# Matrix product with batch normalisation on one core: a fifth chunk copied apart, the last half chunk whole, and other durations in the planner

## The chip, the core and the metric

The kernel runs on one core of a Trainium2 chip. Five engines of that core take part, each with its own queue of instructions that it works off in order: TensorE (PE, with PEld for its weight loads), VectorE (DVE), ScalarE (ACT), GpSimd (POOL) and SyncE (SP, which only issues transfers). The metric is the device time in microseconds; 7 runs of the kernel before have the median 210.38 us.

## The reference

```python
y = np.matmul(x, weight)                       # x (16, 512, 1024) float32, weight (1024, 768)
mean = np.mean(y, axis=(0, 1), keepdims=True)
var = np.var(y, axis=(0, 1), keepdims=True)
y_norm = (y - mean) / np.sqrt(var + eps)
return (gamma * y_norm + beta).astype(np.float32)
```

So 8192 rows of 1024 are multiplied into 768 columns, and each column is normalised by its mean and variance over all 8192 rows. No column can be stored before its last row is computed.

## The kernel before

**Tiles.** The 8192 rows are 16 chunks of 512 (`CH`), called c0 to c15 here. The 768 columns are six blocks of 128, called b0 to b5 (`nt` in the code). K is cut into 8 slices of 128: 4 values of `jw` times 2 of `e`, so one chunk of one block takes 8 matrix instructions.

**Load phase.** GpSimd issues the loads of x (`load_x`, L386), four transfers for a chunk, which turn float32 into bf16 on the way into a buffer called `ring` that holds three chunks. VectorE transposes them into `xT` tiles: L414 moves pairs of bf16 as one float32, so that the two `e` planes stay interleaved; L407, for the chunks in `SINGLE` (c2, c3, c6), moves single bf16 and leaves the planes apart. TensorE computes b0 and b1 with x as the stationary operand (`rows_unit`, L480; two units of 16 instructions for a chunk, each into one PSUM bank) for c0 to c13. For c14 and c15 it does them the other way round (`ga_unit`, L782). Each unit of `rows_unit` is worked off by three engines: ACT squares it (L626), VectorE adds it to `sum1` (L629), ACT keeps it in bf16 (L639), and the square is added either by GpSimd to `sum2` or by VectorE to `sum3` (`add_squares`, L633, both). After the last unit the sums are folded (`tot`, L763 and L768) and a few small matmuls (L840) bring them across the partitions.

**Column blocks.** b2 to b5 have w as the stationary and x as the moving operand (`col_unit`, L545, 8 instructions of 512 columns). c0 to c3 do them in the load phase; c4 to c15 do them after it, block by block, b2 first. The result in PSUM is read by VectorE for its statistics (`bn_stats`, L678) and by ACT, which keeps it in bf16 (L682). When a block has all its chunks, its scale and shift are computed (`finish_tasks`), and eight pieces of 1024 rows are normalised (L1005), turned back (by a transposing transfer, L1107, or on TensorE, L1023) and stored by SP (L1089). The 8 units of PSUM are handed out in turn, so the ninth unit waits until the first one has been kept.

**Copies apart.** `part_chunk` (L517) copies an interleaved `xT` chunk into two planes `x_pl`, four instructions of 128x1024 for a chunk. ACT does that for the chunks in `PARTED` during the load. For the chunks in `LATE` (c12 to c15) it is done by GpSimd or VectorE, whichever the planner picks, once b3 of the last late chunk has been kept; the planes then serve b4 and b5. The twelve `xT` slots are all taken at that time, so a copy goes into the slot of a chunk that has been copied already; the first late chunk (`i == 0`) goes into small free tiles instead. In b3 the late chunks come first, in b4 they come last (`CHUNKS`); a late chunk draws its neighbour of the pair with it.

**The end.** The last block of the last chunk (`last_unit`, L720) is computed in the three pieces of `PIECES` (256, 128 and 128 columns), each with its own statistics (L727) in `fin`. Then come the last scale and shift (L1166 to L1178), the normalisation of b5 (L1201), the turning (L1023), the copy out of PSUM (L1214) and eleven stores (L1217).

**What sets the order.** Nothing runs in the order in which the program names it. Every piece of work is a `task` with a due time, the engines that may do it and for each engine a duration; `arrange` then plays the whole kernel through once while it is built, always gives the engine that is free first the ready task that is due first, and writes the instructions down in that order. Each engine's queue is thus fixed by the durations in the code, and on the chip it is worked off in that order, whatever the durations are there. A task with two engines goes to the one that the planner sees free first. A task with `lock` is kept apart from GpSimd's in the planner when VectorE does it.

Of the kernel before, what the change touches and what calls it, by code (L numbers as in the profile page):

```python
# [227 lines left out]
def kernel(  # L228
# [15 lines left out]
    B, M0, K = x.shape  # L244
# [3 lines left out]
    P = 128  # L248
    NT = N // P
    KQ = K // 4  # L250
    CH = 512
    RT = CH // P
    C = M // CH
    QR = 256
    QPC = CH // QR
    JW = KQ // 64
    PIECES = ((0,QR),(QR,P),(QR+P,P))
    WAKE = 8
    FILL = 2
    EARLY = 4  # L260
# [1 line left out]
    GA = 2  # L262
    NA = GA * P
    GY = 2
    PAD = 34
    HELD = 1
    ASTAT = {2:tuple(range(4,16))}
    RC = C - 2
    XT, YB, SQ = C - EARLY, 27, 3
    ADDED = (0,6,16,28,40)  # L270
    PARTED, LATE, SINGLE = (4,5,7,8,9,10), (12,13,14,15), (2,3,6)
    MODE = {2:'xact',3:('xact',)*7+('pe',),4:'pe'}
    MODE = {nt: m if isinstance(m, tuple) else (m,) * (C // GY) for nt, m in MODE.items()}
    RING = 3 * CH // 32 * KQ // 2
# [46 lines left out]
    tot = singles.tile([P, 2, NA], f32)  # L321
    stats = singles.tile([P, (NT - GA) * C + PAD, 6], f32)
    fin = singles.tile([P, 9 + 6 * len(PIECES)], f32)
    psums = {nt: singles.tile([P, 2, C], f32, name=f"psums{nt}") for nt in ASTAT}
# [20 lines left out]
    def task(prio, engines, emit, deps=(), lock=False, **kw):  # L345
        t = Task(prio, engines, emit, deps, **kw)
        t.lock = lock
        tasks.append(t)
        return t
# [13 lines left out]
    LINE, PER_KB = 0.00119, 1 / 385.0  # L363
# [16 lines left out]
    def load_x(m0, rows, slot):  # L380
        def emit(eng):
            x_bf = piece(slot).bitcast(bf16).rearrange("p (t k) -> p t k", k=KQ)
            slot.tile = x_bf
            src = x_flat[m0:m0 + rows].rearrange("(t r) k -> r t k", r=32)
            for i in range(4):
                seq(nc.gpsimd.dma_start(x_bf[32 * i:32 * i + 32], src[:, :, KQ * i:KQ * (i + 1)]))  # L386
        return emit
# [34 lines left out]
    t = 1.0  # L422
    affine = None
    for kind, n, *n1 in order:
        if kind == "w":
            took = 4 * 192 * 4 * (n1[0] - n) / 4 * PER_KB * 1.024
            w_ready[n] = task(t, {"POOL": (2.0, 2.0)}, load_w(n, *n1), dma=took)
            w_ready[n].count = 4
            t += 2.1 * (n1[0] - n)
            if n1[0] == JW:  # L430
                task(t, {"POOL": (0.6, 0.6)}, lambda eng: make_identity(nc, ident))
            continue
        rows = n1[0] if kind == "p" else QR if kind == "x" else CH
        m0 = n if kind == "p" else n * rows
        if m0 == M // 2:
            affine = task(t, {"SP": (5.0, 7.0)}, load_affine, [x_ready[m0 // CH - 3, 0, JW]])
        slot = Slot(rings, rows // 32 * KQ // 2)
        load = task(
            t, {"POOL": (2.55, 2.55)}, load_x(m0, rows, slot), dma=rows * K * 4 / 1024 * PER_KB * 1.024,
            takes=[slot])  # L440
        load.count = 4
        t += 2.7 * rows / QR
        for i in range(rows // QR):
            c, q = divmod(m0 // QR + i, QPC)
            for j0, j1 in ((0, JW // 2), (JW // 2, JW)) if m0 < CH else ((0, JW),):
                new = q == 0 and j0 == 0
                x_ready[c, q, j1] = task(
                    -1000 + t, dve((2.2 if c in SINGLE else 1.16) * (j1 - j0) / JW + 0.02),
                    turn_x(slot, x_slot[c], m0, i * QR // 32, j0, j1, new), [load],
                    uses=[slot] if new else [slot, x_slot[c]], takes=[x_slot[c]] if new else [])  # L450
                if not new:
                    x_ready[c, q, j1].deps.append(x_ready[c, 0, JW // 2 if m0 < CH else JW])
            x_ready.setdefault((c, q, JW // 2), x_ready[c, q, JW])
        if rows % QR:
            t0 = rows // QR * QR // 32
            m1 = m0 + 32 * t0
            c, q = divmod(m1 // QR, QPC)
            x_ready["tile", m1 // P] = task(
                -1000 + t, dve(0.63), turn_x(slot, x_slot[c], m0, t0, 0, JW, False, P),
                [load, x_ready[c, 0, JW]], uses=[slot, x_slot[c]])  # L460
            x_ready[c, q, JW] = x_ready[c, q, JW // 2] = x_ready["tile", m1 // P]
# [36 lines left out]
    def part_chunk(c, now, engines, small=False, step=0.0, after=()):  # L498

        src = x_slot[c]  # L500
        slots = [Slot(sqs if jw < SQ else ys) for jw in range(JW)] if small else [Slot(xts)] * JW
        ts = []

        def copy(jw):
            def emit(eng):
                if small:
                    if jw < SQ:
                        x_pl = sqpool.tile([P, 2, CH], bf16, tag="sq")
                    else:
                        x_pl = ypool.tile([P, 2, CH], bf16, tag="y")  # L510
                    slots[jw].tile = [x_pl]
                elif jw == 0:
                    x_pl = xtpool.tile([P, JW, 2, CH], bf16, tag="xT")
                    slots[0].tile = [x_pl[:, i] for i in range(JW)]
                dst = slots[jw].tile[0 if small else jw]
                pairs = src.tile[:, jw].rearrange("p m e -> p e m")
                seq(nc.scalar.copy(dst, pairs) if eng == "ACT" else ENG[eng].tensor_copy(dst, pairs))  # L517
            return emit

        for jw in range(JW):  # L520
            new = small or jw == 0
            ts.append(task(
                now + step * jw, engines, copy(jw), [x_ready[c, q, JW] for q in range(QPC)] + list(after) + ([] if new else ts[:1]),
                uses=[src] + ([] if new else [slots[jw]]), takes=[slots[jw]] if new else []))
        plain[c] = slots, ts, small

    def moving(c, jw, e, r0, r1, parted):
# [36 lines left out]
    clock = [12.0]  # L564
# [51 lines left out]
    def rows_stats(c, ts, slot, t):  # L616
        now = clock[0]
        h = ts[0] * P // QR
        sq_slot = Slot(sqs)
        state = {}  # L620
        n = len(ts) * NA

        def square(eng):
            sq_sb = sqpool.tile([P, 2 * NA], f32, tag="sq")
            state["sq"] = sq_sb
            seq(nc.scalar.activation(sq_sb[:, 0:n], slot.tile[:, 0:n], AF.Square))  # L626

        def add_rows(eng):
            seq(nc.vector.tensor_add(sum1, slot.tile[:, 0:n], sum1))  # L629

        def add_squares(eng):
            acc = sum2 if eng == "POOL" else sum3
            seq(ENG[eng].tensor_add(acc, acc, state["sq"][:, 0:n]))  # L633

        def keep(eng):
            if "y" not in y_row[c].__dict__:
                y_sb = ypool.tile([P, RT, NA], bf16, tag="y")
                y_row[c].y = y_sb
            seq(nc.scalar.copy(  # L639
                y_row[c].y[:, ts[0]:ts[0] + len(ts)].rearrange("p s n -> p (s n)"), slot.tile[:, 0:n]))  # L640

        new = ts[0] == 0
        kw = {"uses": [slot] + ([] if new else [y_row[c]]), "takes": [y_row[c]] if new else []}
        up = 0 if c < RC - 1 else now
        a = task(now + 3.0 - up, act(0.494), square, [t], uses=[slot], takes=[sq_slot])
        b = task(now + 3.2 - up, dve(0.608), add_rows, [a], uses=[slot])
        s = task((now + 4.2 if c < RC - 2 else 0), {"POOL": (1.23, 1.28), "DVE": (0.608, 0.7)}, add_squares, [a],
                 True, uses=[sq_slot])
        k = task(now + 3.4, act(0.48), keep, [b], **kw)
        row_end[c, ts[0]] = a, b, s, k  # L650
# [59 lines left out]
    def last_unit(q):  # L710
        nt, c = NT - 1, C - 1
        r0, rows = PIECES[q]
        slot = Slot(banks)
# [420 lines left out]
    for nt in range(GA, NT - 1):  # L1134
        if nt == NT - 2:
            for i, c in enumerate(LATE):
                part_chunk(c, clock[0] + 0.0 + 4.0 * i, {"POOL": (1.3, 1.35), "DVE": (1.1, 1.2)},
                           i == 0, 4.0 / 4, [col_end[NT - 3, late[-1]][1]])
        for c in CHUNKS[nt]:
            for jws in halves if nt > GA or c > EARLY + 2 else [[jw] for jw in range(JW)]:  # L1140
                col_unit(nt, c, jws)
        f = finish_tasks(nt)
        start = clock[0] + 3.0
        for i in range(C // GY):
            if nt == NT - 2 and C // GY - HELD <= i:
                held.append((nt, GY * i, f))
                continue
            col_block(nt, GY * i, start + STEP[nt] * i, f)
# [3 lines left out]
    for c in range(EARLY, C - 1):  # L1152
        for jws in halves:
            col_unit(nt, c, jws)
    for q in range(len(PIECES)):
        last_unit(q)
# [35 lines left out]
    for c, r0, rows in ends:  # L1192
# [5 lines left out]
        for i in range(n):  # L1198
            def norm_part(eng, c=c + i, r0=r0, rows=min(rows, CH)):
# [5 lines left out]
                              uses=[y_of(nt, c + i)]))  # L1205
        m0 = c * CH + r0
        count = rows // P
        b, bank = turn_block(due + 0.6 * (n - 1), nt, m0, count, norms, [y_of(nt, c + i) for i in range(n)])
        slot = Slot(xts)
# [6 lines left out]
        def store(eng, slot=slot, m0=m0, count=count):  # L1216
# [6 lines left out]
             uses=[slot])  # L1223
# [41 lines left out]
```

## Time and profile before

| what | value |
|---|---|
| median of 7 runs | 210.38 us (208.95 to 211.29) |
| the profiled execution | 209.6 us, span 207.8 us |
| busy: PE, DVE, ACT, POOL | 92%, 75%, 70%, 57% of the span |
| granted clock of TensorE | 0.974 of full speed, lower only after 190 us |
| 26 to 93 us (x still loading) | PE busy 66.20 of 67.00 us, DVE 61.53, POOL 54.43, 194 GB/s |
| 93 to 101 us (end of the load) | PE busy 7.65 of 8.00 us, POOL 7.55 |
| 112 to 165 us (b2, b3, b4) | PE busy 52.67 of 53.00 us, DVE 47.41, POOL 34.14, 302 GB/s |
| 165 to 190 us (b5) | PE busy 24.83 of 25.00 us, 305 GB/s |
| L633 on POOL, on DVE | 22 of 1301 ns, 6 of 836 ns |
| L517 on POOL, on DVE | 9 of 1201 ns, 7 of 899 ns |

A line of the timeline gives the start, the length, the engine, the line of the code, the operation and how many equal instructions it joins; in brackets stands how long the engine sat idle before it and for what. A line of the chain of work that ended last gives the start, the length, and what ran. The rates are those of what was moved, and a load is counted by its bf16 side.

### The profile page before, as it was taken

The page shows a single profiled execution, that of the slowest core. Times are in us where ns is not written, and L with a number is a line of the kernel's source. Part 1 is how long each engine was busy: PE and PEld are TensorE (multiplying, and loading weights), DVE is VectorE, ACT ScalarE, POOL GpSimd, SP SyncE. Part 2 cuts the span into 40 slices and gives each one's busy share as a digit, 9 for nine tenths or more (in the row PEclk, how much of TensorE's full clock was granted, in tenths as well). Part 3 has the DMA queues.
Part 4 walks back from the last instruction along what each step waited for, and adds up shares of the span by engine and source line. Part 5 has one row for each costly group of instructions (what it writes and reads, how often), then busy time and mean ns, then how long its engine had stood idle before and what let it go on. Part 6 is the DMA issues. An engine that isn't in the chain of part 4 may idle for free.

```text
span 207.8 us, 3502 instructions
## 1 busy us (share of the span) xinstructions
PE 192.2 (92%) x1217; PEld 117.2 (56%) x1232; DVE 156.1 (75%) x241; ACT 144.6 (70%) x252; POOL 118.4 (57%) x139
## 2 busy tenths in 40 slices
PE   7998989999999999999999999999999999997900
PEld 3465554656588888776865444444444455545900
DVE  4221889999999989878889999589999496248800
ACT  2001561368979999998888777989767969876940
POOL 7987954787499999999303999469830000000000
PEclk9999999999999999999999999999999999999675
DMA  5999999999999999999304898999999999999997
GB/s 64 161 198 189 195 196 196 196 197 196 190 193 197 197 196 195 192 172 188 45 0 156 313 342 306 155 356 341 327 269 280 274 317 325 320 281 347 330 347 238
DMA packets 94082, 47.69 MB, mean 229 GB/s; under 512 B 19824, under 2 KB 93552, under 8 KB 94064
## 3 DMA queue, kind: packets, MB, share of 16 engines
q0 software_dynamic: 34688, 18.36, 64.7%
q1 hardware_dynamic: 59376, 29.11, 51.5%
q8 instruction: 9, 0.15, 0.3%
q14 instruction: 9, 0.07, 0.1%
HBM read 36.71 MB, written 25.17 MB: 298 GB/s over the span
## 4 chain that ended last, share of the span: by engine, by line
PE 75%; DMA 10%; ACT 4%; issue 3%; POOL 2%; DVE 2%; ACTq 0%; DVEq 0%; POOLq 0%
PE y_ps L545 48%; PE y_ps L480 20%; DMA ring<-in_x_dram 8%; ACT o_sb L1214 3%; DMA w_sb<-in_weight_dram 3%; PE y_ps L782 2%; PE o_ps L1023 2%; DVE xT_sb L414 1%; POOL ring L386 1%; PE y_ps L720 1%; POOL tot L768 1%; PE a_ps L887 0%; ACTq L1260 0%; PE o_ps L1053 0%; POOL tot L763 0%
## 5 line engine op out<-in xcount | busy, mean ns | idle before, releaser
L545 PEld LDWEIGHTS <-w_sb 128*128 128x128 bf16 x512 | 49.6, 97 | 57.7
L545 PE MATMUL y_ps<-xT_sb,w_sb 128*128 128x512 bf16 (+1 forms) x255 | 59.3, 377 | 0.5
L545 PE MATMUL y_ps<-x_pl,w_sb 128*128 128x512 bf16 x242 | 57.6, 379 | 0.3
L386 POOL DMA_DIRECT2D ring<-in_x_dram x76 | 47.3, 628 | 12.3 <-DVE xT_sb L407 5.6
L480 PE MATMUL y_ps<-w_sb,xT_sb 128*128 128x256 bf16 x448 | 50.7, 273 | 1.4 <-DVE xT_sb L414 0.8
L480 PEld LDWEIGHTS <-xT_sb 128*128 128x128 bf16 x448 | 43.7, 98 | 9.6 <-issue 1.7
L414 DVE STREAM_TRANSPOSE xT_sb<-ring 128x1024 f32<-128x1024 f32 (+1 forms) x29 | 31.2, 1112 | 13.1 <-DMA ring<-in_x_dram 12.3
L678 DVE BATCH_NORM_STATS2 stats<-y_ps 128x6 f32<-128x512 f32 x46 | 30.8, 683 | 11.4 <-PE y_ps L545 9.7
L682 ACT CAST y_sb<-y_ps 128x512 bf16<-128x512 f32 x51 | 29.1, 589 | 14.2 <-DVE stats L678 8.1
L921 POOL TENSOR_TENSOR ring<-ring,sum 128x1024 f32<-128x1024 f32 (+1 forms) x11 | 23.7, 2177 | 17.1 <-DVE ring L916 16.4
L626 ACT ACTIVATE sq_sb<-y_ps 128x512 f32<-128x512 f32 x28 | 16.9, 608 | 23.5 <-PE y_ps L480 22.2
L633 POOL TENSOR_TENSOR sum<-sum,sq_sb 128x512 f32<-128x512 f32 x22 | 28.6, 1301 | 3.2 <-ACT sq_sb L626 2.4
L517 ACT COPY x_pl<-xT_sb 128x1024 bf16<-128x1024 bf16 x24 | 24.1, 1051 | 1.8 <-DVE xT_sb L414 1.8
L629 DVE TENSOR_TENSOR sum<-y_ps,sum 128x512 f32<-128x512 f32 x28 | 18.9, 675 | 7.9 <-ACT sq_sb L626 6.7
L1023 PE MATMUL o_ps<-ident,y_sb 128*128 128x128 bf16 x136 | 20.1, 241 | 1.7 <-DVE y_sb L1201 1.5
L916 DVE TENSOR_TENSOR ring<-y_sb,a_ps 128x1024 f32<-128x1024 bf16 (+1 forms) x16 | 16.8, 1079 | 2.8 <-DMA out_dram<-ring 2.8
L639 ACT CAST y_sb<-y_ps 128x512 bf16<-128x512 f32 x28 | 15.8, 593 | 3.0 <-DVE sum L629 2.9
L1119 ACT CAST ring<-ring 128x1024 f32<-128x1024 bf16 x15 | 15.7, 1052 | 1.4 <-DMA ring<-y_sb 1.4
L407 DVE STREAM_TRANSPOSE xT_sb<-ring 128x2048 bf16<-128x2048 bf16 x6 | 13.5, 2282 | 0.2 <-DMA ring<-in_x_dram 0.2
L1023 PEld LDWEIGHTS <-y_sb 128*128 128x128 bf16 x136 | 11.7, 109 | 3.3 <-DVE y_sb L1201 1.9
L517 POOL COPY x_pl<-xT_sb 128x1024 bf16<-128x1024 bf16 x9 | 10.5, 1201 | 3.9 <-DVE x_pl L517 3.1
L561 PE MATMUL idle_ps<-idle_sb 128*128 128x512 f32 x20 | 11.2, 717 | 1.5 <-DVE idle_sb L311 1.5
(92 smaller groups left out, 146.7 us busy)
## 6 DMA issues: line engine op xcount, KB each, us to landing
out_dram<-ring SPq DMA_DIRECT2D x38, 512.0 KB, 4.0
ring<-in_x_dram POOLq DMA_DIRECT2D x52, 256.0 KB, 8.5
out_dram<-o_sb SPq DMA_DIRECT2D x6, 512.0 KB, 5.2
ring<-in_x_dram POOLq DMA_DIRECT2D x16, 128.0 KB, 5.1
out_dram<-ring SPq DMA_DIRECT2D x4, 256.0 KB, 3.0
w_sb<-in_weight_dram POOLq DMA_DIRECT2D x8, 96.0 KB, 4.5
w_sb<-in_weight_dram POOLq DMA_DIRECT2D x4, 192.0 KB, 5.1
ring<-in_x_dram POOLq DMA_DIRECT2D x4, 192.0 KB, 8.2
```

Of the source, the lines that this page charges most:

```text
L386: seq(nc.gpsimd.dma_start(x_bf[32 * i:32 * i + 32], src[:, :, KQ * i:KQ * (i + 1)]))
L414: seq(nc.vector.transpose(dst, src[:, :, jw0:jw1]))
L480: seq(nc.tensor.matmul(y_ps[:, s], x_of(c, jw, e, t * P, (t + 1) * P), w_sb[:, jw, e, 0:NA], start=(s == 0 and jw == 0 and e == 0), stop=( ...
L517: seq(nc.scalar.copy(dst, pairs) if eng == "ACT" else ENG[eng].tensor_copy(dst, pairs))
L545: seq(nc.tensor.matmul(y_ps, w_sb[:, jw, e, nt * P:(nt + 1) * P], moving(c, jw, e, q0 * QR, q1 * QR, parted), start=(jw == 0 and e == 0 an ...
L626: seq(nc.scalar.activation(sq_sb[:, 0:n], slot.tile[:, 0:n], AF.Square))
L629: seq(nc.vector.tensor_add(sum1, slot.tile[:, 0:n], sum1))
L633: seq(ENG[eng].tensor_add(acc, acc, state["sq"][:, 0:n]))
L678: seq(nc.vector.bn_stats(dst, slot.tile))
L682: seq(nc.scalar.copy(y(nt, c), slot.tile))
L921: seq(ENG[eng].tensor_add(slot.o, slot.o, row[:, None, :].to_broadcast([P, n, NA])))
L1023: seq(nc.tensor.transpose(dst, src, ident))
```

## The change

Four edits, of which the last touches only numbers that the planner uses:

- `PIECES` has two pieces of 256 columns in place of 256, 128 and 128, so the last half chunk is one piece. `fin` shrinks by one entry of 6 floats, and `PAD` grows the statistics tile by 2 entries.
- `LATE` gets c11 as a fifth member, last in its order. b3 now begins with c10 to c15 and b4 ends with them.
- A copy of `part_chunk` that may go to either engine carries the planner's `lock`.
- The planner's durations: a load costs GpSimd 2.68 us for 512 rows and less for fewer (2.55 for any before); adding squares costs it 1.36 (1.23 before), a late copy 1.1 (1.3 before); VectorE has 0.62 for the squares (0.608) and 0.63 for a late copy (1.1).

```diff
-    PIECES = ((0,QR),(QR,P),(QR+P,P))
+    PIECES = ((0,QR),(QR,QR))
-    PAD = 34
+    PAD = 36
-    PARTED, LATE, SINGLE = (4,5,7,8,9,10), (12,13,14,15), (2,3,6)
+    PARTED, LATE, SINGLE = (4,5,7,8,9,10), (12,13,14,15,11), (2,3,6)
...
         load = task(
-            t, {"POOL": (2.55, 2.55)}, load_x(m0, rows, slot), dma=rows * K * 4 / 1024 * PER_KB * 1.024,
+            t, {"POOL": (2.68 * rows / CH, 2.68 * rows / CH)}, load_x(m0, rows, slot), dma=rows * K * 4 / 1024 * PER_KB * 1.024,
             takes=[slot])
...
                 now + step * jw, engines, copy(jw), [x_ready[c, q, JW] for q in range(QPC)] + list(after) + ([] if new else ts[:1]),
-                uses=[src] + ([] if new else [slots[jw]]), takes=[slots[jw]] if new else []))
+                len(engines) > 1, uses=[src] + ([] if new else [slots[jw]]), takes=[slots[jw]] if new else []))
...
-        s = task((now + 4.2 if c < RC - 2 else 0), {"POOL": (1.23, 1.28), "DVE": (0.608, 0.7)}, add_squares, [a],
+        s = task((now + 4.2 if c < RC - 2 else 0), {"POOL": (1.36, 1.36 + 0.05), "DVE": (0.62, 0.7)}, add_squares, [a],
                  True, uses=[sq_slot])
...
-                part_chunk(c, clock[0] + 0.0 + 4.0 * i, {"POOL": (1.3, 1.35), "DVE": (1.1, 1.2)},
+                part_chunk(c, clock[0] + 0.0 + 4.0 * i, {"POOL": (1.1, 1.15), "DVE": (0.63, 0.7)},
                            i == 0, 4.0 / 4, [col_end[NT - 3, late[-1]][1]])
```

What the built program shows of it: TensorE's order is the same up to the first units of b3. GpSimd adds 21 squares (22 before) and makes 15 late copies (9 before); VectorE adds 7 (6 before) and makes 5 (7 before). In the load phase VectorE's additions stand in other places between its transposes. In b4 the order is now c4 to c10, c12 to c15, and c11 falls behind c4 and half of c5 of b5, because its planes go into the slot of c15's planes, which b4 frees last.

## The prediction

> **What bounds the kernel now.** I read the page first (busy shares), then the chain of work that ended last, then the busy time by stages, and last the timeline of VectorE and GpSimd where the diff moves work.
>
> The chain, piece by piece (start, length, what):
>
> ```profile
> 25.27 1.26 DVE xT_sb L414
> 26.57 1.92 PE y_ps L480 x16
> ...
> 56.52 27.95 PE y_ps L480 x256
> ...
> 100.15 0.73 POOL tot L768
> 100.93 0.61 PE tot_ps L840 x4
> 101.54 4.56 PE y_ps L782 x40
> ...
> 187.84 1.84 PE y_ps L720 x24
> ```
>
> The same by stages (length of the stage, then busy PE, PEld, DVE, ACT, POOL, the granted clock, DMA share, GB/s):
>
> ```profile
> 26.00:93.00 67.00, 66.20 (x491) 48.28 (x496) 61.53 (x69) 52.48 (x82) 54.43 (x68) 1.00 1.47 194
> 93.00:101.00 8.00, 7.65 (x60) 5.67 (x58) 6.00 (x9) 7.15 (x16) 7.55 (x10) 1.00 1.21 161
> 101.00:112.00 11.00, 10.95 (x81) 7.57 (x83) 10.05 (x30) 8.34 (x27) 0.00 (x0) 1.00 0.02 4
> 112.00:165.00 53.00, 52.67 (x247) 23.58 (x250) 47.41 (x64) 43.06 (x82) 34.14 (x20) 1.00 1.08 302
> 165.00:190.00 25.00, 24.83 (x176) 14.02 (x177) 14.84 (x31) 19.36 (x29) 0.00 (x0) 1.00 1.18 305
> ```
>
> TensorE is the bound from 26.57 us, when the second half of c1 is there, to 189.7 us, when the last half chunk is done. The 256 instructions of L480 from 56.52 take 27.95 / 256 = 0.109 us each with no wait between them, though x is loading at 194 GB/s beside them: the planner has filled TensorE with column units and it works off a backlog. The five stages together hold 162.30 us of work in 164.00, so 1.70 us is all that any reordering could win there, and part of that is missing records. Before 26.57 the loads set the time; behind 189.7 a fixed tail follows: from the first of the last stores, issued at 192.38, the stores run at 347 GB/s until 206.57. Neither end is reordered, apart from the last half chunk. So what the change is worth is read from TensorE: which waits it takes from it, which it gives it, and what its own instructions save.
>
> The only clear wait of TensorE in the middle is for the folded squares: in the chain L840 starts at 100.93 behind GpSimd's L768, and TensorE's idle before it is 0.29 us, 0.38 us for its weight load.
>
> VectorE and GpSimd at the end of the load (start, length, engine, line, operation; in brackets the idle time before it):
>
> ```profile
> 73.38 2.37 DVE L414 STREAM_TRANSPOSE xT_sb<-ring 128x1024 f32<-128x1024 f32 x2 [0.82 <-DMA ring<-in_x_dram]
> 75.68 2.25 DVE L629 TENSOR_TENSOR sum<-y_ps,sum 128x512 f32<-128x512 f32 x3
> 77.84 0.68 DVE L633 TENSOR_TENSOR sum<-sum,sq_sb 128x512 f32<-128x512 f32 x1
> 78.72 2.37 DVE L414 STREAM_TRANSPOSE xT_sb<-ring 128x1024 f32<-128x1024 f32 x2 [0.20 <-DMA ring<-in_x_dram]
> 81.02 2.24 DVE L629 TENSOR_TENSOR sum<-y_ps,sum 128x512 f32<-128x512 f32 x3
> 84.08 2.37 DVE L414 STREAM_TRANSPOSE xT_sb<-ring 128x1024 f32<-128x1024 f32 x2 [0.82 <-DMA ring<-in_x_dram]
> ```
>
> These are c10, c11 and c12. VectorE gets to each with 0.2 to 0.8 us to spare, and TensorE needs them soon after: c11 at 81.0 (56.52 + 7 x 3.49), c12 at 86.03. This small slack is what the new order spends.
>
> **The squares in the load phase.** GpSimd makes 21 in place of 22 (1.30 us each), VectorE 7 in place of 6 (0.836 us mean). GpSimd is busy 7.55 of the last 8 us, so one square less ahead of the loads of c12 to c15 moves these up by about 1.3 us and the fold with them. In the new order GpSimd's last square still waits for the square of c13 on ACT (done at 96.2 before, when GpSimd was issuing the last load until 97.09), so the fold gains at most 97.10 - 96.2 = 0.9 us; I take 0.5, because the last load still waits for a transfer to land. Either is over 0.38, so TensorE's wait in front of L840 goes: -0.38 us. What is late next there is the transposes of c15: they end at 103.07 and c15's second half is needed at 101.54 + 3 x 0.87 = 104.2, so 0.38 fits. The loads that come earlier win nothing themselves, as TensorE had no wait for x after 26.57 us. Their four issues each stay the same on GpSimd's queue; only squares move past them.
>
> VectorE has the price. Counted by the built order from c5's transposes (47.07, set by the transfer) to c8's, it has two more L678 (0.61 apart) and one L629 less (0.7): +0.5, so c8 starts at 63.0 (62.68 before). Then one L629 more lies behind c8, and a square stands behind each of c8, c9, c10 and c11; before, only behind c8, c10 and c12. With 2.30 us for two transposes, 0.72 to 0.75 for an L629 and 0.84 for a square: c9 starts at 63.0 + 2.30 + 4 x 0.72 + 0.84 = 69.0 (68.02 before), c10 at 69.0 + 2.30 + 2.24 + 0.84 = 74.4, c11 at 79.7, c12 at 85.1. First halves are ready 1.25 us later: c11 at 81.0, just when it is needed; c12 at 86.35 against 86.03. TensorE waits +0.3 us there. Bounds: 0, if the squares go at the fastest row (0.67: four times 0.17 less); 0.3 + 4 x 0.36 = 1.8 us, if each takes the longest row (1.20). I take 0.3, the mean row. Queued behind c12's units on TensorE is everything else, so this wait is not given back.
>
> **The planner's lock and costs for the late copies.** GpSimd makes 15 in place of 9, VectorE 5 in place of 7. Copies and VectorE's small operations hold each other up:
>
> ```profile
> 147.86 3.01 POOL L517 COPY x_pl<-xT_sb 128x1024 bf16<-128x1024 bf16 x3 [0.70 <-DVE rstd L974]
> 148.84 1.06 DVE L976 SCALAR_TENSOR_TENSOR shift<-tmp,rstd,beta_sb 128x1 f32<-128x1 f32 x1
> 149.93 1.67 DVE L1005 TENSOR_SCALAR y_sb<-y_sb,scale,shift 128x1024 bf16<-128x1024 bf16 x2
> ```
>
> L976 takes 1.06 us beside GpSimd's copies and 0.21 without (167.64). Over the late copies of before I sum an excess of 4.7 us on VectorE (L517 1.45, L975 and L976 1.77, L1005 1.44), 0.52 per GpSimd copy. Six copies more add 3.1, two copies less on VectorE take away 1.4: +1.7 us of VectorE between 141 and 165. It idles 1.56 before its L678 at 163.90 and 1.08 before the one at 165.68, together 2.64, so it has caught up when b4 ends; in between, TensorE has eight PSUM banks of 1.73 us ahead of a lag of at most 5 us now. Cost 0; without that cover up to 1.7. Of the first four copied chunks all are ready 2 us or more before TensorE by my count: GpSimd starts at about 141 and needs 3 x 1.04 to 3 x 1.56 us for a chunk, one VectorE copy beside.
>
> The Trainium skill, page "SBUF — State Buffer", section "SBUF: two separate sides", says that GpSimd and such VectorE operations share one port pair by an exclusive lock, held for the whole instruction; the rows agree in kind. Read at its strongest, each of the 15 VectorE operations concerned would wait a whole copy of 1.04 us: 15.6 us in place of my 7.8, which would put VectorE 7 us behind at the end of b4 and speak against the change. The trace's 0.52 per copy decides for me.
>
> **c11 copied apart.** A unit with interleaved x takes 1.81 us (142.21 to 144.02), one with planes 1.73 (144.02 to 145.74); c11 has one in b4 and one in b5: -0.16. Its GpSimd copies can start only when c15's unit of b4 is done. TensorE has 8 L1023 (0.45), c4 (1.73) and half of c5 (0.86) = 3.04 us until the first half is due, for two copies of 1.04 to 1.56: 0 to 0.1; I take 0. b4's last unit thus falls 2 x 1.73 = 3.5 us later in TensorE's order. From there to the first L1005 took 3.0 us (165.48 to 168.44); TensorE has c6 and c7 of b5 meanwhile (3.45), so 0.4 us of slack; the first stored piece comes about 1 us later than now and the second 1 us earlier, since 16 L1023 now run in a row. SP has two transposing transfers (L1107) moved ahead of all these stores, and no store waits for a new event. Cost 0.
>
> **The last half chunk.** 8 instructions of 0.113 and 16 of 0.0575 (1.83 us) become 16 of 0.113 (1.81): -0.02. The last statistics cover 256 columns, 0.42 (L789) in place of 0.30 us, on the path: +0.12, and one shorter L1166: 0. Together +0.1.
>
> **Sum.** -0.38 + 0.3 - 0.16 + 0.1 = -0.14, within what can be seen of no change (a measurement of this kernel tells about 0.5%, 1.05 us). The profiled execution (209.6, of which 207.8 span) would become 209.5; it lies 0.8 under the median of the 7 runs. On the median: 210.2.
>
> **The rivals.**
> 1. *VectorE is later in the load than I walk* (slower). Place: c11 and c12 in front of TensorE. For it: VectorE is busy 61.53 of 67 us, the planner puts a square at 0.62 that measures 0.84, and one waited 1.14 us for ACT. Against it: transfers leave 0.2 to 0.8 us before each chunk. Price by the longest row: +1.5, 211.7. It is slower by over 0.5% from a wait of 1.5 us on.
> 2. *The lock puts VectorE behind at the end of b4* (slower): beyond the 2.64 us of idle plus 0.4, each us is a wait of TensorE in front of the 16 L1023. With 0.8 per copy in place of 0.52: 15 x 0.8 - 4.7 - 1.4 = 5.9, less 3.0: +2.9, 213.1. Against it: the L678 between, most of VectorE's work there, keep their 0.68 us beside the copies.
> 3. *The new plan meets its waits* (faster): all idle time of TensorE in 26 to 190 us goes, 1.70, and c11's 0.16: 208.5; half of it, 209.3. For it: durations nearer to the measured ones. Against it: 0.80 of the 1.70 is spread over 67 us without a wait of that size.
> 4. *It does nothing that shows*: waits of 0 in the load, -0.46: 209.9; it joins my forecast.
>
> **How the numbers follow.** Forecast with rival 4: 0.62; rival 1: 0.14; rival 2: 0.08; rival 3: 0.16. The range reaches half way into rival 3 and to the price of rival 1: 209.2 to 211.9. Faster 0.16, same 0.62, slower 0.22.
>
> **What would show it.** Right: no idle in front of L840; c12's L414 about 1 us later than 84.08 and a short wait of L480 on L414; TensorE without a wait from 112 to 188; 16 L720 over 1.81 us. Wrong: a wait of TensorE over 1 us for L414, or for L1005 in front of L1023 near 171; or a last store ending over 1 us away from 206.6.

## The result, and the profile after

| | before | after |
|---|---|---|
| median | 210.91 us (60 runs, 208.95 to 213.99) | 209.44 us (25 runs, 208.26 to 211.31) |
| ratio, 95% interval | | 0.9944 (0.9927 to 0.9961) |
| profiled execution | 209.6 us, span 207.8 | 209.25 us, span 207.5 |

The changed kernel is faster by 0.56%, or 1.2 us (0.8 to 1.5). The forecast was 210.2 us, 0.14 less than the median of the 7 runs known then (210.38): the time lies inside the range, by 0.24 us, but the gain is eight times the sum that was worked out. That the time fits the range is luck: the 60 runs of before have the median 210.91, and from there the same sum would have given 210.8 and a range that starts at 209.7, above the measured 209.44. The ratios here and below compare undisturbed executions alone, while the medians are over all; one profiled execution further down (c11_part, 213.84 us) was disturbed, and only its rows before 101 us are used.

The chain of work that ended last, after (start, length, what):

```profile
25.83 1.25 DVE xT_sb L414
27.13 1.92 PE y_ps L480 x16
...
57.08 27.95 PE y_ps L480 x256
...
98.05 2.72 PE y_ps L782 x24
100.77 0.79 PE tot_ps L840 x8
101.56 4.56 PE y_ps L782 x40
...
187.49 1.83 PE y_ps L720 x16
189.34 0.44 DVE fin L727
```

TensorE's backlog is the chain again, but GpSimd's fold (L763, L768) has left it: L840 is now one group of eight in 0.79 us where it was two groups with L768 in front of the second. The head came 0.56 us later in this execution (27.13 against 26.57), by the loads of the first chunks; in a second execution of the same kernel (all_again) it came at 26.46. So the gain is read from 27.13 to the first L720: 160.36 us, against 161.27 before.

Busy time by stages, after (length of the stage, then busy PE, PEld, DVE, ACT, POOL, the granted clock, DMA share, GB/s):

```profile
26.00:93.00 67.00, 65.93 (x488) 47.77 (x491) 61.96 (x70) 52.27 (x83) 54.33 (x68) 1.00 1.48 195
93.00:101.00 8.00, 7.95 (x65) 6.13 (x63) 6.88 (x10) 7.39 (x15) 6.61 (x9) 1.00 1.15 154
101.00:112.00 11.00, 10.95 (x82) 7.58 (x84) 9.65 (x30) 8.59 (x27) 0.00 (x0) 1.00 0.01 3
112.00:165.00 53.00, 52.71 (x249) 23.83 (x252) 47.89 (x62) 42.20 (x80) 39.01 (x25) 1.00 1.08 296
165.00:190.00 25.00, 24.59 (x167) 13.81 (x168) 15.07 (x32) 19.70 (x30) 2.07 (x2) 1.00 1.17 334
```

Between 93 and 101 us TensorE is busy 7.95 of 8.00 us (7.65 before) and GpSimd 6.61 (7.55 before). Between 112 and 165 us GpSimd has 4.9 us more of copies and VectorE two copies fewer; all in all VectorE is busy for 0.48 us more (47.89 against 47.41), and TensorE loses nothing.

VectorE and GpSimd at the end of the load, after (start, length, engine, line, operation; in brackets the idle time before it):

```profile
76.57 2.24 DVE L629 TENSOR_TENSOR sum<-y_ps,sum 128x512 f32<-128x512 f32 x3
78.73 0.68 DVE L633 TENSOR_TENSOR sum<-sum,sq_sb 128x512 f32<-128x512 f32 x1
79.44 2.37 DVE L414 STREAM_TRANSPOSE xT_sb<-ring 128x1024 f32<-128x1024 f32 x2
83.64 2.57 POOL L386 DMA_DIRECT2D ring<-in_x_dram  x4
83.90 0.68 DVE L633 TENSOR_TENSOR sum<-sum,sq_sb 128x512 f32<-128x512 f32 x1
84.79 2.37 DVE L414 STREAM_TRANSPOSE xT_sb<-ring 128x1024 f32<-128x1024 f32 x2 [0.21 <-DMA ring<-in_x_dram]
86.22 2.64 POOL L633 TENSOR_TENSOR sum<-sum,sq_sb 128x512 f32<-128x512 f32 x2
88.82 2.45 POOL L386 DMA_DIRECT2D ring<-in_x_dram  x4
...
96.67 1.28 POOL L633 TENSOR_TENSOR sum<-sum,sq_sb 128x512 f32<-128x512 f32 x1 [0.48 <-ACT sq_sb L626]
```

GpSimd takes turns, one load and two squares, 5.18 us from load to load (83.64 to 88.82), and VectorE's square at 83.90 falls in the 2.57 us in which GpSimd only issues a load. In the order of before, squares of both engines run at the same time; the experiments come back to this. The lines of the late copies, after:

```profile
142.88 10.46 POOL L517 COPY x_pl<-xT_sb 128x1024 bf16<-128x1024 bf16 x9
149.01 0.88 DVE L975 TENSOR_TENSOR scale<-rstd,gamma_sb 128x1 f32<-128x1 f32 x1
150.05 2.39 DVE L1005 TENSOR_SCALAR y_sb<-y_sb,scale,shift 128x1024 bf16<-128x1024 bf16 x2
```

As before, VectorE's small operations are long beside GpSimd's copies (L975 takes 0.16 us without them, at 170.74).

### The profile page after: what moved, and what is told of

It is laid out like the page before. It is cut to its first block, busy times and chain, and to the rows that moved or that the text cites. A ratio compares the mean times of both kernels' runs of the same rounds, so it can differ in the third digit from the quotient of the medians.

```text
span 207.5 us, 3484 instructions
## 1 busy us (share of the span) xinstructions
PE 191.7 (92%) x1209; PEld 115.9 (56%) x1224; DVE 156.3 (75%) x239; ACT 143.5 (69%) x251; POOL 123.8 (60%) x144
## 4 chain that ended last, share of the span: by engine, by line
PE 78%; DMA 10%; ACT 4%; issue 1%; DVE 1%; POOL 1%; ACTq 0%; DVEq 0%; POOLq 0%
PE y_ps L545 49%; PE y_ps L480 21%; DMA ring<-in_x_dram 8%; PE y_ps L782 4%; ACT o_sb L1214 3%; DMA w_sb<-in_weight_dram 3%; PE o_ps L1023 2%; PE y_ps L720 1%; POOL ring L386 1%; DVE xT_sb L414 1%; PE a_ps L887 0%; ACTq L1260 0%; PE o_ps L1053 0%; PE tot_ps L840 0%; POOL w_sb L377 0%
## 5 line engine op out<-in xcount | busy, mean ns | idle before, releaser
L545 PE MATMUL y_ps<-x_pl,w_sb 128*128 128x512 bf16 x257 | 60.6, 379 | 0.3
L545 PE MATMUL y_ps<-xT_sb,w_sb 128*128 128x512 bf16 (+1 forms) x240 | 54.7, 376 | 0.5
L480 PE MATMUL y_ps<-w_sb,xT_sb 128*128 128x256 bf16 x448 | 50.7, 273 | 1.1 <-DVE xT_sb L414 0.8
L480 PEld LDWEIGHTS <-xT_sb 128*128 128x128 bf16 x448 | 43.7, 98 | 9.4 <-issue 1.7
L682 ACT CAST y_sb<-y_ps 128x512 bf16<-128x512 f32 x51 | 28.2, 594 | 11.0 <-DVE stats L678 9.3
L626 ACT ACTIVATE sq_sb<-y_ps 128x512 f32<-128x512 f32 x28 | 16.3, 607 | 23.0 <-PE y_ps L480 22.5
L633 POOL TENSOR_TENSOR sum<-sum,sq_sb 128x512 f32<-128x512 f32 x21 | 26.9, 1281 | 3.3 <-ACT sq_sb L626 2.6
L629 DVE TENSOR_TENSOR sum<-y_ps,sum 128x512 f32<-128x512 f32 x28 | 18.9, 675 | 8.5 <-ACT sq_sb L626 7.2
L517 POOL COPY x_pl<-xT_sb 128x1024 bf16<-128x1024 bf16 x15 | 17.4, 1199 | 6.8 <-PE y_ps L545 3.9
L639 ACT CAST y_sb<-y_ps 128x512 bf16<-128x512 f32 x28 | 15.8, 600 | 8.0 <-DVE sum L629 7.8
L1023 PE MATMUL o_ps<-ident,y_sb 128*128 128x128 bf16 x136 | 16.5, 220 | 1.7 <-DVE y_sb L1201 1.6
L561 PE MATMUL idle_ps<-idle_sb 128*128 128x512 f32 x20 | 12.0, 761 | 1.5 <-DVE idle_sb L311 1.5
L1023 PEld LDWEIGHTS <-y_sb 128*128 128x128 bf16 x136 | 9.6, 98 | 4.0 <-DVE y_sb L1201 2.0
```

The source lines that it names most:

```text
L480: seq(nc.tensor.matmul(y_ps[:, s], x_of(c, jw, e, t * P, (t + 1) * P), w_sb[:, jw, e, 0:NA], start=(s == 0 and jw == 0 and e == 0), stop=( ...
L545: seq(nc.tensor.matmul(y_ps, w_sb[:, jw, e, nt * P:(nt + 1) * P], moving(c, jw, e, q0 * QR, q1 * QR, parted), start=(jw == 0 and e == 0 an ...
L682: seq(nc.scalar.copy(y(nt, c), slot.tile))
L1023: seq(nc.tensor.transpose(dst, src, ident))
```

## The experiments

**The parts one by one, and two by two.** Theory 1 was the prediction's own, without its price: the wait in front of L840 goes, the two units of c11 save 0.16 us, and nothing is paid. Theory 2: the gain comes from c11 and the store stream. Theory 3: the single last piece is itself a gain. all_again is the changed kernel itself. Seven kernels fill the table of all combinations; before_again is the one without any part.

load_plan has only these two lines changed:

```diff
-            t, {"POOL": (2.55, 2.55)}, load_x(m0, rows, slot), ...
+            t, {"POOL": (2.68 * rows / CH, 2.68 * rows / CH)}, load_x(m0, rows, slot), ...
-        s = task(..., {"POOL": (1.23, 1.28), "DVE": (0.608, 0.7)}, add_squares, [a],
+        s = task(..., {"POOL": (1.36, 1.36 + 0.05), "DVE": (0.62, 0.7)}, add_squares, [a],
```

> Only the planner's durations of the load phase (2.68 us for a load, 1.36 and 0.62 for adding squares); GpSimd adds 21 squares, VectorE 7; late copies and last piece as before. Theory 1 (the wait in front of L840 goes and the load costs nothing for it): 0.4 to 0.6 us faster, L840 without idle time, and no wait of TensorE for L414 at c12. The prediction's own walk: 0.1 us faster, with 0.3 us of wait at c12. Theory 2 (the gain is at the stores and the late copies): within 0.2 us of before.

c11_part has only the fifth late chunk, the lock and the durations of a late copy:

```diff
-    PARTED, LATE, SINGLE = (4,5,7,8,9,10), (12,13,14,15), (2,3,6)
+    PARTED, LATE, SINGLE = (4,5,7,8,9,10), (12,13,14,15,11), (2,3,6)
...
+                len(engines) > 1, uses=[src] + ...
-                part_chunk(c, ..., {"POOL": (1.3, 1.35), "DVE": (1.1, 1.2)},
+                part_chunk(c, ..., {"POOL": (1.1, 1.15), "DVE": (0.63, 0.7)},
```

> Only c11 as the fifth late chunk, with the lock and the planner's durations of a late copy; GpSimd makes 15 late copies, VectorE 5. Theory 1: 0.16 us faster by the two units with planes, 0.4 at most. Theory 2 (moving c11 to the end of b4 and its transposing transfers in front of the stores fills the hole in the store traffic at 180 to 184 us, so that the tail is shorter too): 0.6 to 1.0 us faster, last store ends 0.5 us or more earlier behind the first L1217 than before. A lock that bites would show as up to 2.9 us slower.

one_piece has only the last half chunk changed:

```diff
-    PIECES = ((0,QR),(QR,P),(QR+P,P))
+    PIECES = ((0,QR),(QR,QR))
-    PAD = 34
+    PAD = 36
```

> Only the last half chunk as one piece, with the larger statistics tile. The prediction: 0.1 us slower (matrix instructions -0.02, last statistics +0.12). Theory 3 (the single piece is itself a gain: one statistics step and one chain of semaphores less on the path between the last matrix instruction and the first store): 0.2 to 0.4 us faster.

> The changed kernel as it is, beside the three parts on the same chip. Every theory expects the difference measured first, -1.2 us (0.9944 of before, 0.9927 to 0.9961). If the parts are independent, the three kernels that do one part each add up to it; if they add up to less, the parts need each other.

The other four, in a second group: before_again (no edit), and the changed kernel with one part undone, by the same lines read backwards.

> The kernel before, profiled once more, to see whether its first profiled execution was a typical one. Theory 1, sharpened by the three parts (GpSimd has no idle time left in the last 10 us of the load, so every delay there reaches L840, and the profile shown before caught it at its smallest): L840's wait and the gap between the end of L782 x24 and the start of L782 x40 differ by more than 0.5 us from the 0.38 us of the first profile, and the execution is longer by about as much. Rival (the waits in front of L840 that c11_part and one_piece show come from those edits): the same 0.4 us again. Time 210.9 us, ratio 1.000.

> The changed kernel with the load phase's durations as before; c11 and the single piece stay. Theory 1: it loses most of the gain: 0.1 to 0.2 us faster than before (210.7 to 210.8), idle time in front of L840 of 0.4 to 1.8 us. Rival, the gain is in the late copies and the stores: it keeps 0.8 us or more (under 210.1).

> The changed kernel with the last half chunk in the three pieces of before. Theory 1: as fast as the changed kernel or 0.05 to 0.1 us faster (209.3 to 209.5). Rival, the single piece is worth something of its own (32 instructions less on TensorE and its weight loads, shorter code): 0.3 us or more slower than the changed kernel (209.8).

> The changed kernel without c11 as a late chunk, late copies as before. Theory 1: 0.16 us slower than the changed kernel (209.6), no wait in front of L840. Rival, c11 and the store stream are half of the gain: 0.5 to 0.7 us slower than the changed kernel (210.0).

Measured (medians of 12 runs; before had 210.93 us beside the first four and 211.20 beside the last four, 35 runs each):

| kernel | load plan | c11 | piece | median | less than before | ratio, 95% interval |
|---|---|---|---|---|---|---|
| before_again | | | | 211.30 | -0.10 | 1.0003 (0.9969 to 1.0036) |
| load_plan | x | | | 210.06 | 0.87 | 0.9983 (0.9958 to 1.0009) |
| c11_part | | x | | 210.64 | 0.29 | 0.9981 (0.9948 to 1.0014) |
| one_piece | | | x | 210.55 | 0.38 | 0.9997 (0.9970 to 1.0023) |
| no_load_plan | | x | x | 210.80 | 0.40 | 0.9993 (0.9958 to 1.0028) |
| load_and_c11 | x | x | | 209.81 | 1.39 | 0.9951 (0.9926 to 0.9976) |
| load_and_piece | x | | x | 210.47 | 0.73 | 0.9994 (0.9967 to 1.0021) |
| all_again | x | x | x | 209.39 | 1.54 | 0.9930 (0.9902 to 0.9959) |

Each part's worth is the mean of its four steps in the table, with 0 for the kernel without any. By the medians: the load plan (0.87 + 1.10 + 0.35 + 1.14) / 4 = 0.87 us, c11 (0.29 + 0.52 + 0.02 + 0.81) / 4 = 0.41, the piece (0.38 - 0.14 + 0.11 + 0.15) / 4 = 0.13. By the ratios, taken as shares of 211 us: the load plan (0.36 + 0.63 + 0.06 + 1.33) / 4 = 0.60, c11 (0.40 + 0.68 + 0.08 + 1.35) / 4 = 0.63, the piece (0.06 - 0.23 - 0.25 + 0.44) / 4 = 0.01. Single ratios are uncertain by some 0.6 us. So the times say that the load plan and c11 both count, not which counts more, and that the piece is not distinct from 0. Neither of the two is clear of the noise without the other: the intervals of load_plan, load_and_piece, c11_part and no_load_plan all reach 1, and only those of load_and_c11 and all_again, which have both, lie below it.

Theory 1 fits no_load_plan (ratio 0.9993, and idle time in front of L840), but not the other prices. load_plan was expected 0.4 to 0.6 us faster and came 0.87 faster by the median, 0.36 by the ratio; load_and_c11 came at 209.81, the rival's figure; load_and_piece was expected at 209.6, by the rival at 210.0, and came at 210.47. The single piece was to cost 0.1 us, and that does not show either. What the traces show is firmer than these times.

**Where the load plan's gain lies.** The executions' traces give it stage by stage. TensorE's orders are the same up to b3 in all eight kernels (c11_part is left out here), so that the distance between the same two starts is the same work plus waits. The shortest distances are 15.70 us from the first L480 of c8 to that of c12, and 14.84 from there to the first L782 behind L840. What goes beyond them is wait; beside it stand the longest squares (L633) on each engine:

| execution | wait c8 to c12 | wait c12 to L782 | longest square GpSimd | VectorE | first L480 of c1's second half |
|---|---|---|---|---|---|
| before | 0.00 | 0.53 | 1.79 | 1.20 | 26.57 |
| before_again | 0.74 | 0.16 | 1.46 | 1.75 | 26.60 |
| one_piece | 0.09 | 1.73 | 1.80 | 0.91 | 26.76 |
| no_load_plan | 0.00 | 1.06 | 1.77 | 1.71 | 27.60 |
| load_plan | 0.38 | 0.01 | 1.31 | 0.69 | 26.28 |
| load_and_c11 | 0.00 | 0.00 | 1.30 | 0.69 | 27.64 |
| load_and_piece | 0.60 | 0.00 | 1.31 | 0.69 | 27.35 |
| after | 0.00 | 0.00 | 1.30 | 0.69 | 27.13 |
| all_again | 0.40 | 0.00 | 1.31 | 0.69 | 26.46 |

With the old plan the wait in front of L840 and L782 is anything from 0.16 to 1.73 us (mean of four 0.87); with the new one it is 0 five times of five. The wait at c11 and c12 is much the same in both (mean 0.21 and 0.28).

The summary of line L633 shows what is different: least, median and greatest duration in ns. First before_again, then after:

```profile
L633 POOL TENSOR_TENSOR sum<-sum,sq_sb x22: 1269/1280/1460, 23.0 to 97.5; 128x512 f32<-128x512 f32 x22
L633 DVE TENSOR_TENSOR sum<-sum,sq_sb x6: 667/754/1754, 21.8 to 95.1; 128x512 f32<-128x512 f32 x6
```

```profile
L633 POOL TENSOR_TENSOR sum<-sum,sq_sb x21: 1269/1277/1296, 22.7 to 96.7; 128x512 f32<-128x512 f32 x21
L633 DVE TENSOR_TENSOR sum<-sum,sq_sb x7: 681/682/693, 21.3 to 94.9; 128x512 f32<-128x512 f32 x7
```

A square alone takes 0.68 us on VectorE and 1.28 on GpSimd. In the old plan squares of both engines run at the same time (they meet) three or four times in each of the four executions, in the new plan not once in the five. The timeline of before_again (GpSimd's group is two squares; the second starts at 78.54 by the trace), with TensorE behind it:

```profile
77.17 2.63 POOL L633 TENSOR_TENSOR sum<-sum,sq_sb 128x512 f32<-128x512 f32 x2
78.60 1.75 DVE L633 TENSOR_TENSOR sum<-sum,sq_sb 128x512 f32<-128x512 f32 x1
81.57 3.67 PE L480 MATMUL y_ps<-w_sb,xT_sb 128*128 128x256 bf16 x32 [0.57 <-ACT sq_sb L626]
```

and of one_piece (the second squares of GpSimd's two groups start at 78.81 and at 94.62):

```profile
77.44 3.12 POOL L633 TENSOR_TENSOR sum<-sum,sq_sb 128x512 f32<-128x512 f32 x2
78.76 0.68 DVE L633 TENSOR_TENSOR sum<-sum,sq_sb 128x512 f32<-128x512 f32 x1
...
93.26 3.17 POOL L633 TENSOR_TENSOR sum<-sum,sq_sb 128x512 f32<-128x512 f32 x2
94.61 0.69 DVE L633 TENSOR_TENSOR sum<-sum,sq_sb 128x512 f32<-128x512 f32 x1 [0.49 <-ACT sq_sb L626]
...
98.52 2.88 PE L782 MATMUL y_ps<-xT_sb,w_sb 128*128 128x256 bf16 x24 [0.73 <-DVE xT_sb L414]
102.41 0.61 PE L840 MATMUL tot_ps<-ones,tot 128*128 128x1 f32 x4 [0.67 <-POOL tot L768]
```

The engine that starts second takes longer by most of what is left of the other's square. In before_again GpSimd was first by 0.06 us, and VectorE's square took 1.75 us: c11's transposes came late and TensorE waited 0.57 us. In one_piece VectorE was first, by 0.05 and 0.01 us, and two of GpSimd's squares took 1.75 and 1.80 (in c11_part, with the same order, 1.76 and 1.76): the last loads and the fold came late, and TensorE waited 0.73 and 0.67 us. So some hundredths of a microsecond decide whether VectorE pays, at c11, or GpSimd, whose loads and squares have little idle time left (7.55 us busy of 8 in the first profile). The wait in front of L840 and L782 is largest where GpSimd's squares lost most: its lengthened squares lost 0.51 us against 1.28 each in before, 0.18 in before_again, 0.99 in one_piece and 0.49 in no_load_plan, and TensorE waited 0.53, 0.16, 1.73 and 1.06 (in before_again it had already lost 0.74 at c11). All four make the same 22 squares on GpSimd.

The planner keeps squares apart (they have the lock), but by its own durations. With the new ones all four of VectorE's squares between 68 and 84 us fall beside loads of GpSimd on the chip (68.64, 73.68, 78.73 and 83.90 in after). This is not because the new numbers are nearer to the chip: a turn of one load and two squares takes GpSimd 5.18 us, and the planner put it at 2.55 + 2 x 1.23 = 5.01 before and at 2.68 + 2 x 1.36 = 5.40 after.

**Doses.** Three kernels put time back into the changed one, at one place, with every order as it was. extra_pool1 and extra_pool2 add GpSimd copies behind its squares of c10, extra_dve one on VectorE behind its square of c9:

```diff
-            seq(ENG[eng].tensor_add(acc, acc, state["sq"][:, 0:n]))
+            seq(ENG[eng].tensor_add(acc, acc, state["sq"][:, 0:n])); eng == "POOL" and c == 10 and seq(nc.gpsimd.tensor_copy(state["sq"][:, 0:n], state["sq"][:, 0:n]))
```

> The changed kernel, with one instruction more on GpSimd: behind its squares of c10 it copies a 128x512 tile of float32 onto itself (estimate 0.65 to 1.3 us: half of a whole L633, as it reads one tile in place of two). All orders are otherwise the same. Theory 1 (GpSimd's chain of loads and squares sets when x and the folded squares come; in the changed kernel it has 0.5 us of idle time before its last load and 0.2 in front of L840): waits of TensorE of 0 to 0.6 us come back in front of L782 or L840; 0 to 0.6 us slower than the changed kernel. Rival (the gain is in the order of VectorE or in TensorE's own instructions): no wait and the same time.

> The same with two such copies in a row. Theory 1: what goes beyond the 0.7 us of slack arrives in full, so 0.6 to 1.9 us slower than the changed kernel (210.0 to 211.3), with a wait in front of L840 or L782 of that size, as in the kernel before. Rival: the same time as the changed kernel.

> The changed kernel, with one copy of a 128x512 float32 tile onto itself more on VectorE, behind its square of c9, ahead of the transposes of c11 (estimate 0.35 to 0.7 us). It measures what VectorE's lateness costs, which the prediction put at 0.3 us of wait at c12. If VectorE has no slack left there: slower by the copy, 0.35 to 0.7 us, with the wait of L480 for L414 at c11 or c12. If the prediction's small slack is in truth larger (squares on VectorE take 0.68 us and not 0.84): 0 to 0.2 us slower.

A fourth shows which of the two durations does it; it is the changed kernel with the old numbers for the squares:

```diff
-        s = task(..., {"POOL": (1.36, 1.36 + 0.05), "DVE": (0.62, 0.7)}, add_squares, [a],
+        s = task(..., {"POOL": (1.23, 1.28), "DVE": (0.608, 0.7)}, add_squares, [a],
```

> The changed kernel with the squares' durations in the planner as before; only the load's 2.68 us is new. GpSimd has 21 squares and VectorE 7 here too, but GpSimd's stand 3, 1, 3, 2, 1 between the last loads in place of 2, 2, 2, 2, 2, and L840 stands behind 10 more L782. Theory 1: GpSimd's time is what counts, so no wait in front of L840, and 0 to 0.4 us from the changed kernel; an uneven order may make one load late. Rival (the even spread is the gain): 0.5 to 0.9 us slower than the changed kernel.

| kernel (before beside them: 211.02 us) | added | median | ratio, 95% interval | wait c8 to c12 | wait in front of L840 and L782 |
|---|---|---|---|---|---|
| extra_pool1 | 0.61 us on GpSimd | 209.26 | 0.9926 (0.9897 to 0.9955) | 0.38 | 0.00 |
| extra_pool2 | 1.63 us on GpSimd | 209.85 | 0.9971 (0.9933 to 1.0009) | 0.00 | 0.33 |
| extra_dve | 0.47 us on VectorE | 209.52 | 0.9934 (0.9901 to 0.9967) | 0.66 | 0.00 |
| load_cost_only | | 209.77 | 0.9951 (0.9919 to 0.9983) | 0.00 | 0.00 |

In the timeline of extra_pool2:

```profile
83.01 1.63 POOL L633 COPY sq_sb<-sq_sb 128x512 f32<-128x512 f32 x2
...
100.81 0.61 PE L840 MATMUL tot_ps<-ones,tot 128*128 128x1 f32 x4 [0.17 <-POOL tot L768]
```

The first 0.61 us on GpSimd is free: its 0.5 us of idle time, which in after stands before its last square, and the slack in front of L840 take it. The second copy brings the wait for L768 back, and the median rises by 0.6 us from extra_pool1 to extra_pool2. That the wait is only 0.33 us in the profiled execution, where 0.6 to 1.9 were expected, puts the slack of this one execution at about 1.3 us and not 0.7. VectorE's 0.47 us cost nothing in the median (1.50 us under before, against 1.54 for all_again), so there was slack too. Its trace has 0.66 us of wait, in the execution with the earliest head of all (25.70); how much of that is the copy's is not shown. load_cost_only keeps most of the gain, with 21 squares on GpSimd, spread 3, 1, 3, 2, 1; its L840 only stands later among the L782 (3.63 us behind the first of them in place of 2.72), which is work and no wait. Two of its squares on VectorE still met GpSimd's and took 0.89 and 1.29 us, though its turn, 2.68 + 2 x 1.23 = 5.14, is the nearest to the chip's 5.18; none of GpSimd's was lengthened. Whether the even spread is worth anything is not shown: 1.25 us under before, against 1.54 for all_again, and the intervals overlap.

GpSimd thus comes earlier to the fold for two reasons: it has one square (1.28 us) less, and none of its squares is lengthened (0.18 to 0.99 us in the old plan). Every kernel with the new load number has both, and no run parts them.

## Why the prediction was right or wrong

1. **TensorE is the bound, and only its waits and its own work count: right.** From 112 to 165 us it stayed busy for 52.71 of 53.00 us, and the two ends did not move but for the head, which comes between 25.70 and 27.84 us in thirteen profiled executions (26.57 and 26.60 in two of before, 27.13 and 26.46 in two of the changed kernel).

2. **"TensorE's wait in front of L840 goes: -0.38 us": right in kind, too small.** It went in every execution with the new plan. Its size was that of one execution. By the distances it is 0.53 us there; other executions with the old load plan show 0.16, 1.06 and 1.73, depending on which engine's square was lengthened where, and the mean of four is 0.87. This is the term that was mis-sized most. The execution with 0.53 (0.38 by the idle rows) was one of the quicker ones, 0.8 us under its median, as the prediction noted without asking why.

3. **"VectorE has the price ... +0.3": the step that failed.** A wait of that size is there (0.28 us on the mean of five), but it is no price of the change: the old plan has 0 to 0.74 us in the same place, 0.21 on the mean of four. The walk put the new order's transposes of c11 at 79.7 and c12 at 85.1; they started at 79.44 and 84.79 in after, 79.64 and 85.00 in all_again, and those of c12 were held up by their transfer (0.21 and 0.23 us), not by VectorE's work. Each square was costed at 0.84 us, the mean of six rows. Three of them were lengthened: 0.89 and 1.20, which started while GpSimd was in a square, and 0.90, for which no meeting shows. The other three took 0.67 and 0.68. The new order separates the two engines, and all seven take 0.68 to 0.69. By extra_dve's median another 0.47 us on VectorE can be borne.

4. **The lock at the late copies, cost 0: right.** VectorE's added time was 0.48 us, where 1.7 were allowed for, and the 16 L1023 at 172.11 follow the unit before them without a wait. The Trainium skill's page "SBUF — State Buffer", section "SBUF: two separate sides", was weighed there alone. It says that a VectorE operation with two inputs in SBUF and a GpSimd operation that reads SBUF exclude each other, and that the first to start holds the ports for its whole instruction. The place where these runs show this most plainly is the load: of two squares that start within 0.06 us of each other, the second takes 0.5 us longer beside VectorE's 0.68, or 1.07 longer beside GpSimd's 1.27, so by all but 0.1 to 0.2 us of the first. L629, which reads one operand from PSUM, keeps 2.24 to 2.25 us for three beside GpSimd's squares in all these rows.

5. **c11's planes, -0.16, and no cost at the end of b4 and at the stores: right for TensorE.** From the first L887 (the first blocks' scale and shift spread over the partitions) to the first L720 the four executions with c11 in the table of waits take 78.77 or 78.78 us, the five without 78.93 to 79.18. The part's 0.41 or 0.63 by the times is more; some of the difference, about 0.35 us in the two kernels with the load plan and without c11, is told in the last section, and the rest is open.

6. **The last half chunk, +0.1: right.** L720 takes 1.83 us in place of 1.84, and from the start of the last statistics (L727) to the first normalisation (L1201) it is 1.60 us (189.34 to 190.94) in place of 1.50 (189.71 to 191.21): +0.09. TensorE has 8 matrix instructions less (1217 to 1209), not the 32 that load_and_c11's expectation names.

The sum by measured terms is -0.87 (L840) + 0.07 (c8 to c12) - 0.16 + 0.09 = -0.87 us; measured was 1.2 (0.8 to 1.5). The rest, 0.3 us, is within the scatter. Rival 3, "the new plan meets its waits", is nearest to what happened, and 0.16 was too small a chance for it. (Half of its 1.70 + 0.16 us is 209.45 and not 209.3; rival 4 adds up to -0.44 and not -0.46.) What was said for it, durations nearer to the measured ones, does not hold for GpSimd's turn (5.01 before, 5.40 after, 5.18 on the chip). What the order itself changes, which operations of the two engines meet, was not asked. Rival 1 had the right place and the wrong sign, and rival 2 did not come.

## What to carry to other kernels

Where operations of two engines lengthen each other, a mean duration holds the meetings of the old order; read least, median and greatest, and ask of an edit that moves either engine which meetings it ends or makes. Where a chain has no idle time, one profile is one draw of its waits: if the profiled execution is faster than the median, the typical wait may be larger than the one shown (0.87 against 0.53 us here). A planner that keeps engines apart in its own times need not do so on the chip: look in the trace whether they are apart, as here numbers that were further off for GpSimd's turn gave the better order. And a table of parts needs the interval of each entry: two ways to read the same runs gave 0.87 and 0.41 us, or 0.60 and 0.63.

## What was not expected of the hardware

- Which of two engines pays for a meeting is decided by some hundredths of a microsecond: in the same orders VectorE's square took 0.68 us and GpSimd's 1.75 to 1.79 (before, one_piece), or VectorE's took 1.75 beside GpSimd's 1.27 (before_again). The time shows as a longer instruction, not as idle time, so that no list of waits names it.
- In the two kernels with the new load plan and without c11 (load_plan, load_and_piece) the span ends 1.60 and 1.61 us behind the last stored byte; in the other executions 1.24 to 1.27. GpSimd's part of the last step of synchronisation took 0.37 us there, 0.08 in before and after. It is about 0.35 us of what these two kernels lack against the full change. In these two alone the trace has a transfer of instructions (8192 bytes) that starts at the very end of the span (207.50 and 209.20 us). Whether it has to do with the wait is not shown.
- With c11 apart and the last half chunk in three pieces (load_and_c11) the stores end 14.85 us behind SP's first instruction for L1217, against 14.50 to 14.65 in the other executions. There the single piece may give back more than its 0.1 us of statistics cost. It is one execution, and the cause stays open.

No version that was tried is faster than the changed kernel by more than the scatter.
